# A Strassen unit in each branch projection, banded attention folded into one block, one-instruction gelu

## The chip, the cores and the metric

The program runs on one core of a Trainium2 chip. Its time is device microseconds of that core, from the runs shown beside the kernel; the profile is one further execution, recorded instruction by instruction. TensorE (PE) multiplies matrices into PSUM, VectorE (DVE) and ScalarE (ACT) do elementwise work, GpSimd (POOL) small work and some transfers, and SyncE (SP) issues most transfers from main memory.

## The reference

Two layers, 256 positions, width 2048, all in float32. Cut to what is computed:

```python
for l in range(DEPTH):                                  # 2
    h = rms_norm(x, mix_norm[l])                        # x: 256 x 2048
    q, k, v, uv, gate_logits = split(h @ w_in[l])       # 1024, 256, 256, 2048, 4096 columns
    q = apply_rope(rms_norm(q, q_norm[l])); k = apply_rope(rms_norm(k, k_norm[l]))
    # 16 query heads and 4 key heads of 64; a query sees the 128 positions up to itself
    a = sliding_window_attention(q, k, v, sinks[l]) @ w_attn_branch[l]      # 1024 x 2048
    u, v = split(gelu(uv))                              # gelu in its tanh form
    v = layer_norm of v in 8 groups of 128
    b = (u * (tril(w_spatial) @ v + bias)) @ w_sgu_branch[l]                # 1024 x 2048
    g = sigmoid(gate_logits)
    x = x + (g[:, :2048] * a + g[:, 2048:] * b) @ w_out[l]
    h2 = rms_norm(x, ffn_norm[l])
    x = x + (silu(h2 @ w_gate[l]) * (h2 @ w_up[l])) @ w_down[l]             # 5632 wide
```

In a block of 128 queries, query i sees the keys j > i of the block before and j <= i of its own: exactly one of the two for each j.

## The kernel before

The 256 positions are two tiles of 128. Every large product goes over *chunks* of 512 output columns, and within a chunk over *halves* of the weight, 256 rows by 512 columns (one 512 KB load). A number is carried as a sum of two fp32r parts: ACT makes `whi` from the loaded half (line 244), DVE makes `wlo` as the rest (line 245), and the left side has `uh` and `ul` in the same way. Each product of 128 rows takes three matmuls, `uh*whi`, `uh*wlo`, `ul*whi` (lines 340 and 341), so a half for both position tiles is 12 matmuls of 512 columns.

Most chunks run as pairs (`pair`). In the first 512 rows of a pair (unit `WINO`, in some pairs two units) the 2x2 blocks are multiplied by a Strassen scheme: seven products P1 to P7 of 6 matmuls in place of eight, at the price of three differences of weights (line 229), seven splits instead of four, sums of the left side (`sums`, split into `sh` and `sl` by the function `finished`, lines 501 to 505) and the copies and additions of lines 362 to 371. The head of a pair (its P products but P3) is interleaved with the last halves of the plan ahead of it. Before the change the in-projection, the output projection, and both parts of the feed-forward have such pairs; the two branch projections, 1024 rows to 2048 columns each, run as four single chunks each.

The list `entries` fixes the order of all halves and products. `Stream.next` runs ahead of it: loads up to seven entries ahead on SP's queue, differences six, splits four ahead into four `hi` and four `lo` buffers. PE's order is the order written; the other engines are ordered by a planner that has a timeline of its own. `tick()` passes once for each 12 matmuls (one *slot*); `after(n, fn)` has `fn` issued n slots later, behind the latest split on DVE. All smaller work is placed by such numbers: attention scores 17 slots after the first half of the queries is there, and so on.

Tiles of 4 KB a partition (left sides, gates, queries, sums, P5's `kept`) come from one pool, `big`, of 25; a tile is given back when its last reader is done. PSUM has four banks for products (`ps_acc`), two for transposes (`ps_tr`) and two for attention (`ps_at`).

A left side is made by `transposed`: DVE transposes 32x32 blocks into a `box` (line 410; one box, a pool of its own), 16 transfers gather it into `tt` (line 416, on POOL's or SP's queue), and ACT and DVE split it (lines 435 and 436, or the steps of `wino`, placed by tuples such as `WINO_HID`). Some go through PE instead (line 453).

Attention (class `Attention`): `scores` multiplies keys by queries (line 754; 128 key columns for the first tile of positions, 256 for the second), adds the mask (758), takes the maximum (762), and ACT takes the exponentials (771). Five slots later `weights` transposes them on PE (783) and ACT copies them out (785); three slots later `values` multiplies by V (793), with the weights as stationary side and 64 columns of V moving, and DVE divides by the sum (797). The result `att` is transposed by `transposed`. Gelu (`Spatial.gelu`, lines 816 to 822) is a square, two DVE instructions and a tanh, on half of the value.

Of the kernel before, what the change touches and what calls it, by code (L numbers as in the profile page):

```python
# [38 lines left out]
WINO_HID = 7, 8, 17, 18, 19, 20  # L39
# [5 lines left out]
TT = 1  # L45
K_TURN = 7
Q_TURN = 7
Q_FIRST = 17
Q_STEP = 5
# [4 lines left out]
GELU_A = 0.044715  # L54
GELU_C = 0.7978845608028654
# [3 lines left out]
def hybrid_trunk(ctx: ExitStack, tc: tile.TileContext, x, mix_norm, w_in, q_norm, k_norm, sinks,  # L59
# [6 lines left out]
    big = ctx.enter_context(tc.tile_pool(name="big", bufs=25))  # L66
# [3 lines left out]
    turned = ctx.enter_context(tc.tile_pool(name="turned", bufs=TT))  # L70
# [26 lines left out]
    class Plan:  # L97


        def __init__(self, key, head, body):  # L100
            self.key, self.head, self.body = key, head, body
            self.left = len(head) + len(body)
            self.paired = bool(head)
# [17 lines left out]
    def single(key, w):  # L121

        return Plan(key, [], [half(w, h, "X") for h in range(w.shape[0] // (2 * P))])

    def pair(key, wa, wb, by_unit=False, last_later=False, two=False):
# [25 lines left out]
        if last_later:  # L151
            body = g[:3] + p3 + g[3:4] + u[:2] + g[4:] + u[2:]
# [7 lines left out]
    plans = []  # L160
    for l in range(DEPTH):
# [21 lines left out]
    for p in plans:  # L183
        if p.head:
            h, n = p.head, min(6 if len(p.head) == 6 else 9, len(ahead.body))
# [5 lines left out]
            elif n == 6:  # L191
                order = [t[0], h[0], t[1], h[1], t[2], t[3], h[3], h[2], t[4], h[4], t[5], h[5]]
            else:
                order = [h[0], t[0], h[1], t[1], h[3], h[2], t[2], h[4], t[3], h[5]]
            if n != 9:
# [7 lines left out]
    class Stream:  # L203
# [7 lines left out]
        def load(self, upto):  # L211
            while self.asked < min(upto, len(entries)):
                for key, w, h, tag in entries[self.asked]["loads"]:
                    raw = (slot([P, 2, CW], name="raw") if tag == "slot" else
                           wraw.tile([P, 2, CW], F32, tag=tag, name=nm("raw"), bufs=None if tag == "raw" else 1))
                    src = w[2 * h * P:2 * (h + 1) * P, :].rearrange("(k p) n -> p k n", p=P)
                    if self.raws:
                        self.loaded = nc.sync.dma_start(raw, src)
                    else:
                        for i in range(2):  # L220
                            self.loaded = nc.sync.dma_start(raw[:, i:i + 1], src[:, i:i + 1])
# [101 lines left out]
    def banks(p, which):  # L323
        if which not in p.acc:
            other = p.paired and p.key[0] != "in" and which == "a"
# [77 lines left out]
    def turn(dst, src, queue):  # L403


        box = turned.tile([P, 4, 4, NT, B], F32, tag="box", name=nm("box"))
# [103 lines left out]

    class Norm:
# [42 lines left out]
    for c in range(NCH):  # L554
# [4 lines left out]
    mask = const.tile([P, S], F32, name="mask")  # L559
    nc.gpsimd.memset(mask, 0.0)  # L560
    nc.gpsimd.affine_select(mask[:, :P], mask[:, :P], pattern=[[1, P]], base=0, channel_multiplier=-1,
                            compare_op=ALU.is_gt, fill=-1e30)
    nc.gpsimd.affine_select(mask[:, P:], mask[:, P:], pattern=[[-1, P]], base=0, channel_multiplier=1,
                            compare_op=ALU.is_ge, fill=-1e30)
    cs = const.tile([P, NT, HD // 2], F32, name="cs")
# [97 lines left out]
    def fetch_large(pl):  # L663
        for n, i in ((13, 2), (17, 3), (21, 0), (25, 1)):
            after(n, lambda i=i: pl.fetch(i))
        after(40, pl.spatial)

    class Attention:


        def __init__(self, pl):
            self.pl = pl
            self.qT = [None] * 2
            self.att = [None] * 2
            self.attT = [None] * 2
            self.live = {}
# [38 lines left out]
        def keys(self, kv):  # L715
# [4 lines left out]
            after(K_TURN, lambda: turn(self.kT, kd.rearrange("p t n a d -> p t (n a d)"), nc.sync))  # L720

        def queries(self, c, q):
            self.rotate(q, NQ // 2, self.pl.rope[0], None)
            self.qT[c] = slot([P, 4, S], name="qT")
            self.att[c] = slot([P, NT, CW], name="att")
            after(Q_TURN, lambda: self.turn_queries(c, q))
            n = Q_FIRST + (4 * Q_STEP - 8) * c
            for t in range(NT):
                for g in (2 * c, 2 * c + 1):
                    after(n, lambda t=t, g=g: self.scores(t, g))  # L730
                    n += Q_STEP
            after(n + 6, lambda: transposed(self.attT, c, self.att[c], queue=nc.sync))
# [12 lines left out]
        def scores(self, t, g):  # L745
            nk = P * (t + 1)
            mk = mask[:, P:] if t == 0 else mask
# [295 lines left out]
```

## Time and profile before

| | us |
|---|---|
| median of 3 runs | 2461.22 (2460.16 to 2461.9) |
| the profiled execution | 2457.45 |
| its span, first to last instruction | 2455.7 |
| PE busy in the span | 2438.1 (99%) |
| DVE busy | 1999.5 (81%) |
| ACT busy | 1472.5 (60%) |

A group of instructions is given as line, engine, operation, output<-inputs, shape, count, then busy time, mean ns of one, and the idle time ahead of it with what ended it. Matmuls are pipelined: one lasts some 390 ns from start to end, but the next starts well before, so the pace is read from starts. DMA moved 506.74 MB, a mean of 206 GB/s.

### The profile page before, as it was taken

To read this page: it belongs to the slowest core of one execution; us is meant where nothing else is said; L and a number is where in the kernel's file an instruction comes from. 1 tells how busy PE (TensorE), PEld (TensorE's weight loads), DVE (VectorE), ACT (ScalarE), POOL (GpSimd) and SP (SyncE) were. 2 spreads that over 40 slices of the span, in tenths; PEclk is the share of its full clock that TensorE was granted. 3 is DMA by queue.
4 is the path that set the end of the run, shared out by engine and by line. 5 is a ranking of instruction groups with operands and counts; after the bars stand their busy time and mean duration, and the time that the engine had idled before them with its cause. 6 is when DMAs were issued, how large, how long until landed. Compare 5 with 4: busy or idle time off the path is not lost.

```text
span 2455.7 us, 31363 instructions
## 1 busy us (share of the span) xinstructions
PE 2438.1 (99%) x10968; PEld 2012.6 (82%) x10968; DVE 1999.5 (81%) x2320; ACT 1472.5 (60%) x1842; POOL 315.6 (13%) x592
## 2 busy tenths in 40 slices
PE   9999999999999999999999999999999999999999
PEld 7888888888888888887887888888888888888877
DVE  6798676797978997899877986768878789978996
ACT  5567544576655665566655665545666556655664
POOL 3100002132210111001101000021322101110110
PEclk9999999999999999999999999999999999999999
DMA  9555657576667657665747446675767675667654
GB/s 299 196 187 163 212 198 220 186 236 210 220 217 233 210 176 231 230 203 170 229 155 257 152 157 223 202 215 177 246 202 236 204 245 189 200 209 241 203 179 139
DMA packets 280782, 506.74 MB, mean 206 GB/s; under 512 B 28272, under 2 KB 40144, under 8 KB 280624
## 3 DMA queue, kind: packets, MB, share of 16 engines
q1 hardware_dynamic: 262544, 486.35, 61.0%
q0 software_dynamic: 17760, 18.12, 2.8%
q8 instruction: 86, 1.41, 0.2%
q14 instruction: 72, 0.59, 0.1%
q10 hardware_dynamic: 320, 0.27, 0.0%
HBM read 475.27 MB, written 2.10 MB: 194 GB/s over the span
## 4 chain that ended last, share of the span: by engine, by line
PE 90%; DVE 3%; DMA 3%; SPq 1%; issue 1%; ACT 1%; DVEq 0%; ACTq 0%
PE acc L340 59%; PE acc L341 29%; DMA raw<-in_w_in_dram 2%; DVE wlo L245 2%; SPq L416 1%; ACT whi L244 1%; PE po L793 1%; PE psc L754 0%; PE ppt L783 0%; DVE raw L229 0%; PE psg L871 0%; PE pt L453 0%; DMA raw<-in_w_up_dram 0%; DMA raw<-in_w_down_dram 0%; DVE box L410 0%
## 5 line engine op out<-in xcount | busy, mean ns | idle before, releaser
L244 ACT ACTIVATE whi<-raw 128x1024 fp32r<-128x1024 f32 (+1 forms) x1074 | 1132.0, 1059 | 883.0 <-PE acc L341 623.4
L245 DVE TENSOR_TENSOR wlo<-raw,whi 128x1024 fp32r<-128x1024 f32 (+1 forms) x1075 | 1301.3, 1219 | 399.0 <-ACT whi L244 386.7
L340 PE MATMUL acc<-whi,uh 128*128 128x512 f32 x2994 | 1170.3, 391 | 1.2 <-ACT uh L439 1.2
L340 PE MATMUL acc<-wlo,uh 128*128 128x512 f32 x2994 | 1167.1, 390 | 3.0 <-DVE wlo L245 2.9
L341 PE MATMUL acc<-whi,ul 128*128 128x512 f32 x2994 | 1166.4, 390 | 0.0
L340 PEld LDWEIGHTS acc<-wlo,uh 128*128 128x128 f32 x2994 | 562.6, 188 | 123.2 <-DVE wlo L245 6.0
L340 PEld LDWEIGHTS acc<-whi,uh 128*128 128x128 f32 x2994 | 562.6, 188 | 117.7 <-ACT uh L439 1.4
L341 PEld LDWEIGHTS acc<-whi,ul 128*128 128x128 f32 x2994 | 562.3, 188 | 117.8 <-DVE ul L444 0.5
L416 POOL DMA_DIRECT2D tt<-box x544 | 266.5, 497 | 1697.0 <-ACT whi L244 695.5
L229 DVE TENSOR_TENSOR raw<-raw,raw 128x1024 f32<-128x1024 f32 x236 | 287.8, 1219 | 1.6 <-DMA raw<-in_w_up_dram 0.8
L341 PE MATMUL acc<-whi,sl 128*128 128x512 f32 x472 | 184.0, 390 | 3.2 <-DVE sl L485 3.2
L340 PE MATMUL acc<-whi,sh 128*128 128x512 f32 x472 | 184.8, 392 | 1.7 <-ACT acc L364 1.7
L340 PE MATMUL acc<-wlo,sh 128*128 128x512 f32 x472 | 184.2, 390 | 0.0
L341 PEld LDWEIGHTS acc<-whi,sl 128*128 128x128 f32 x472 | 88.6, 188 | 22.5 <-DVE sl L485 4.0
L340 PEld LDWEIGHTS acc<-whi,sh 128*128 128x128 f32 x472 | 88.6, 188 | 20.9 <-ACT acc L364 2.1
L340 PEld LDWEIGHTS acc<-wlo,sh 128*128 128x128 f32 x472 | 88.7, 188 | 18.0
L366 DVE TENSOR_TENSOR kept<-acc,kept 128x512 f32<-128x512 f32 x94 | 64.3, 684 | 10.1 <-PE acc L341 10.1
L369 ACT ACTIVATE acc<-kept 128x512 f32<-128x512 f32 x94 | 54.9, 586 | 4.3 <-DVE kept L366 4.2
L888 DVE SCALAR_TENSOR_TENSOR xs<-acc,xs 128x512 f32<-128x512 f32 (+1 forms) x66 | 42.0, 668 | 8.4 <-PE acc L341 8.1
L436 DVE TENSOR_TENSOR ul<-tt,uh 128x512 fp32r<-128x512 f32 x52 | 34.0, 684 | 2.9 <-ACT uh L435 2.9
L435 ACT ACTIVATE uh<-tt 128x512 fp32r<-128x512 f32 x52 | 29.8, 618 | 9.4 <-DMA tt<-box 9.4
L312 POOL TENSOR_TENSOR rv<-ve,neg_half 128x4 f32<-128x4 f32 x8 | 11.9, 1486 | 172.9 <-DVE ve L839 159.5
(137 smaller groups left out, 874.8 us busy)
## 6 DMA issues: line engine op xcount, KB each, us to landing
raw<-in_w_in_dram SPq DMA_DIRECT2D x239, 512.0 KB, 4.7
raw<-in_w_gate_dram SPq DMA_DIRECT2D x176, 512.0 KB, 4.4
raw<-in_w_up_dram SPq DMA_DIRECT2D x176, 512.0 KB, 4.9
raw<-in_w_down_dram SPq DMA_DIRECT2D x176, 512.0 KB, 5.0
raw<-in_w_out_dram SPq DMA_DIRECT2D x64, 512.0 KB, 5.0
tt<-box POOLq DMA_DIRECT2D x544, 32.0 KB, 4.2
raw<-in_w_attn_branch_dram SPq DMA_DIRECT2D x32, 512.0 KB, 5.6
raw<-in_w_sgu_branch_dram SPq DMA_DIRECT2D x32, 512.0 KB, 4.4
```

The costliest lines, as they stand in the source:

```text
L229: self.last = nc.vector.tensor_tensor(out=self.raws[d], in0=self.raws[x], in1=self.raws[y], op=ALU.subtract)
L244: self.high = nc.scalar.activation(hi[:, i, :], raw[:, i, :], AF.Copy)
L245: self.last = nc.vector.tensor_tensor(out=lo[:, i, :], in0=raw[:, i, :], in1=hi[:, i, :].bitcast(F32), op=ALU.subtract)
L340: nc.tensor.matmul(ps, a, part[:, kk, :], start=first and kk + n == 0, stop=False, skip_group_check=True)
L341: nc.tensor.matmul(ps, b, hi[:, kk, :], start=False, stop=kk == 1, skip_group_check=True)
L366: nc.vector.tensor_tensor(out=p.kept[:, int(tag == "P7"), :], in0=a[1], in1=p.kept[:, 1, :], op=ALU.add)
L369: nc.scalar.activation(ps, p.kept[:, t, :], AF.Copy)
L416: q.dma_start(dst[j * B:(j + 1) * B, i], box[i * B:(i + 1) * B, j])
L435: nc.scalar.activation(h, s_, AF.Copy)
L436: nc.vector.tensor_tensor(out=l, in0=s_, in1=h.bitcast(F32), op=ALU.subtract)
L793: nc.tensor.matmul(po[:, h, :], pT[kb][:, h, :], self.kv[:, kb, KVW + g * HD:KVW + (g + 1) * HD], start=kb == 0, stop=kb == t)
L888: nc.vector.scalar_tensor_tensor(out=xs[:, t, sl], in0=sums[t][:, i * w:(i + 1) * w], scalar=scale, in1=xs[:, t, sl], op0=ALU.mult, op1=AL ...
```

## The change

- **Strassen in the branches.** The first two chunks of the attention branch become a pair, and so do those of the gating branch. The left side of the attention branch gets its Strassen sums in a new function `summed`, that of the gating branch through `transposed` with `WINO_FIRST`. Gate chunks 5 and 6 now run ahead of the gating branch's pair.
- **Attention.** For the second tile of positions the two key blocks are merged into one block of 128: ACT copies the own block's scores, DVE overwrites with the earlier block's where the mask says so. Maximum, exponentials and transposes work on 128 columns for either tile. The weights are divided by their sum while untransposed. `values` takes 64 columns of V as the stationary side and moves 512 columns (4 heads) of transposed weights; two key heads write the lower and the upper 64 rows of one PSUM bank. V of the second block is replaced by its difference to the first, and the weights are multiplied by a 0/1 mask for that product. The result is already transposed, so `transposed` falls away; the rows of `w_attn_branch` are loaded in the order of heads that this gives, in two transfers for a half (`rows_of`).
- **Gelu** is one ACT instruction a tile (`Gelu_apprx_tanh`), four in a row for v and four for u, chained behind the exponentials on ACT.
- **Boxes** come from `big`, which has 26 tiles, and the pool `turned` is gone.
- **Placement.** New slots for scores, values, gelu, the mixing with `w_spatial` and its transposes (now 34 slots into a layer, 40 before); queues and delays of some `transposed` calls; Strassen sums of the last feed-forward round end 15 slots after the turn (`WINO_END`) and not 20.

```diff
-WINO_HID = 7, 8, 17, 18, 19, 20
+WINO_HID = 11, 12, 17, 18, 19, 20
+WINO_END = 9, 10, 12, 13, 14, 15
...
-Q_FIRST = 17
-Q_STEP = 5
+W_TURN = 9
+SCORES = (17, 22, 27, 32), (37, 42, 47, 52)
+V_GELU, V_STEP = 4, 6
+U_GELU, U_MIX, U_TURN = 2, (3, 9), (32, 39)
+VALUES = (34, 44), (54, 64)
...
-    big = ctx.enter_context(tc.tile_pool(name="big", bufs=25))
+    big = ctx.enter_context(tc.tile_pool(name="big", bufs=26))
...
+    def rows_of(raw, w, h):
+        if w.shape[0] != QW or not any(w is a for a in by_heads):
+            return [(raw, w[2 * h * P:2 * (h + 1) * P, :].rearrange("(k p) n -> p k n", p=P))]
+        rows = w.rearrange("(c a k d) n -> c a d k n", c=2, a=2, d=HD)
+        k = 2 * (h % 2)
+        return [(raw[a * HD:(a + 1) * HD], rows[h // 2, a, :, k:k + 2]) for a in range(2)]
...
         if last_later:
-            body = g[:3] + p3 + g[3:4] + u[:2] + g[4:] + u[2:]
+            body = g[:2] + p3 + u[:2] + g[2:] + u[2:]
...
-        plans += [single(("att", l), w) for w in cols_of(w_attn_branch[l], NCH)]
-        sgu = [single(("sgu", l), w_sgu_branch[l, :, j * CW:(j + 1) * CW]) for j in range(NCH)]
-        plans += [sgu[0], pair(("in", l), of_in("gate", 5), of_in("gate", 6)), sgu[1], sgu[2],
-                  single(("in", l), of_in("gate", 7)), sgu[3]]
+        plans += [pair(("att", l), c_[0], c_[1])] + [single(("att", l), w) for w in c_[2:]]
+        plans[-3].first = True
+        c_ = cols_of(w_sgu_branch[l], NCH)
+        plans += [pair(("in", l), of_in("gate", 5), of_in("gate", 6)), pair(("sgu", l), c_[0], c_[1]),
+                  single(("in", l), of_in("gate", 7)), single(("sgu", l), c_[2]), single(("sgu", l), c_[3])]
...
-        box = turned.tile([P, 4, 4, NT, B], F32, tag="box", name=nm("box"))
+        box = slot([P, 4, 4, NT, B], name="box")
...
+    def summed(units, c, at):
+        uh, ul = units[c]
+        flat = slot([P, 4, S], name="flat")
+        nc.vector.tensor_tensor(out=flat, in0=uh.bitcast(F32), in1=ul.bitcast(F32), op=ALU.add)
+        ss = slot([P, 4, 2, P], name="sums")
...
-        after(40, pl.spatial)
+        after(34, pl.spatial)
...
-                nc.vector.tensor_tensor(out=pr[:, :, j, :nk], in0=pscore[:, :, :nk],
-                                        in1=mk.unsqueeze(1).to_broadcast([P, 2, nk]), op=ALU.add)
+                mk = mask.unsqueeze(1).to_broadcast([P, 2, P])
+                if t == 0:
+                    nc.vector.tensor_tensor(out=pr[:, :, j, :], in0=pscore[:, :, :P], in1=mk, op=ALU.add)
+                else:
+                    nc.scalar.activation(pr[:, :, j, :], pscore[:, :, P:], AF.Copy)
+                    nc.vector.copy_predicated(pr[:, :, j, :], mk.bitcast(mybir.dt.uint32), pscore[:, :, :P])
...
-            after(5, lambda: self.weights(t, g, pr4, rd))
+            after(4, lambda: nc.vector.tensor_tensor(out=pr4, in0=pr4, in1=rd.unsqueeze(2).to_broadcast([P, 4, P]),
+                                                     op=ALU.mult))
+            after(W_TURN, lambda: self.weights(t, g, pr4))
...
+            nc.scalar.activation(pT[0][:, g % 2], pt, AF.Copy)
+            if t == 1:
+                nc.vector.tensor_tensor(out=pT[1][:, g % 2], in0=pt, in1=causal.unsqueeze(1).to_broadcast([P, 4, P]),
+                                        op=ALU.mult)
...
+            po = ps_at.tile([P, 4, P], F32, tag="at", name=nm("po"))
+            pT = self.pT[t, c]
+            for k in range(t + 1):
+                for a in range(2):
+                    v = (1 - k) * KVW + (2 * c + a) * HD
+                    nc.tensor.matmul(po[a * HD:(a + 1) * HD], self.kv[:, 0, v:v + HD], pT[k][:, a],
+                                     start=k == 0, stop=k == t)
+            uh, ul = (x[:, :, t * P:(t + 1) * P] for x in units)
+            nc.scalar.activation(uh, po, AF.Copy)
+            nc.vector.tensor_tensor(out=ul, in0=po, in1=uh.bitcast(F32), op=ALU.subtract)
...
+            last = self.att.exps
+            for dst in both:
+                for t in range(NT):
+                    with tc.issue_after(last.ins):
+                        last = nc.scalar.activation(dst[:, t, :], dst[:, t, :], AF.Gelu_apprx_tanh)
...
-                pe, soon = c == len(hT) - 1 == 2, c == 3
+                pe, soon = c == len(hT) - 1 == 2, c == 3 or c == 1 and len(hT) == 3
```

More of the change, by code (lines that the diff above doesn't have):

```diff
@@ L324, in banks @@
         if which not in p.acc:
-            other = p.paired and p.key[0] != "in" and which == "a"
+            other = p.paired and p.key[0] != "in" and which == "a" and not p.first
             if other or p.key[0] == "in":
@@ L940, in hybrid_trunk, with gated @@
         for chunks in FIRST_PART[l]:
+            if chunks == FIRST_PART[l][-1]:
+                after(1, lambda: summed(att.attT, WINO, (1, 2, 4)))
             projected(*chunks)
-        for j in range(NCH):
-            ps = product(("att", l))
+        def gated(j, ps):
             ga = gates[j]
@@ L949, in hybrid_trunk @@
                                                op0=ALU.add, op1=ALU.mult)
+        product_pair(("att", l), lambda ps: gated(0, ps), lambda ps: gated(1, ps))
+        for j in range(2, NCH):
+            gated(j, product(("att", l)))
             tick()
```

173 lines of the change are left out of this document (93 added, 80 removed).

## The prediction

> **What bounds the kernel now.** I read the page first, its busy times and the chain that ended last, then the groups by form, then TensorE's waits, and last single stretches of the timeline. The page's first lines and its chain:
>
> ```profile
> span 2455.7 us, 31363 instructions
> PE 2438.1 (99%) x10968; PEld 2012.6 (82%) x10968; DVE 1999.5 (81%) x2320; ACT 1472.5 (60%) x1842; POOL 315.6 (13%) x592
> PE 90%; DVE 3%; DMA 3%; SPq 1%; issue 1%; ACT 1%; DVEq 0%; ACTq 0%
> ```
>
> TensorE is busy for 99% of the span and carries 90% of the chain, so time changes by what its queue loses or gains, and by its waits. A matmul lasts 390 ns but overlaps the next one, so I take the pace from starts, in a quiet stretch of the timeline of TensorE:
>
> ```profile
> 599.78 0.39 PE L341 MATMUL acc<-whi,ul 128*128 128x512 f32 x1
> ...
> 611.80 0.39 PE L340 MATMUL acc<-wlo,uh 128*128 128x512 f32 x1
> ```
>
> From the first to the last of these are 53 steps in 12.02 us: 0.2268 us for a matmul of the large products. Counting the lists of the code gives 10398 of these, 2358 us of the span. The other 98 us are attention, transposes, the start and waits. TensorE's longest waits in total (us, times, longest):
>
> ```profile
> PE acc L341 <- DVE sl L485: 3.2, 2, 1.6
> PE acc L340 <- DVE wlo L245: 2.9, 5, 0.8
> PE ppt L783 <- DVE wsT L654: 2.4, 1, 2.4
> PE acc L340 <- ACT acc L364: 1.7, 1, 1.7
> PE acc L340 <- ACT uh L439: 1.2, 1, 1.2
> ```
>
> They are short: no engine but TensorE bounds a stage for long. The nearest to it is DVE in the attention stretch, as the table by windows shows (columns: PE, PEld, DVE, ACT, POOL busy, granted clock, DMA share, GB/s):
>
> ```profile
> 140.00:160.00 20.00, 20.00 (x100) 16.40 (x99) 19.97 (x39) 12.77 (x22) 4.09 (x2) 1.00 0.47 145
> 280.00:300.00 20.00, 20.00 (x90) 16.39 (x89) 10.18 (x11) 8.83 (x11) 0.00 (x0) 1.00 0.65 221
> 340.00:360.00 20.00, 20.00 (x90) 16.53 (x90) 16.45 (x17) 11.16 (x12) 0.00 (x0) 1.00 0.39 120
> 1340.00:1360.00 20.00, 17.57 (x86) 14.41 (x85) 16.80 (x32) 12.76 (x23) 0.51 (x1) 0.91 0.55 192
> ```
>
> **The change part by part**, on TensorE first. All sums are made against the profiled execution, 2457.45 us (span 2455.7); the median of the runs, 2461.2, lies 3.8 above it, which I add at the end.
>
> *Strassen.* A pair replaces eight products of 6 matmuls by seven. Two more pairs in each of two layers: 4 x 6 = 24 matmuls fewer, 24 x 0.2268 = **-5.4**.
>
> *Transposes of the weights.* For the second tile of positions each group of 8 becomes one of 4. The group of lines of `values`, and the timeline of TensorE:
>
> ```profile
> L793 PE MATMUL po<-kv,pT 128*128 128x64 f32 x192 | 23.1, 270 | 0.0
> ```
>
> ```profile
> 134.00 0.66 PE L783 MATMUL ppt<-ident,pr 128*128 128x128 f32 x4
> ...
> 149.16 1.14 PE L754 MATMUL psc<-kT,qT 64*128 64x256 f32 x8
> 150.24 1.09 PE L783 MATMUL ppt<-ident,pr 128*128 128x128 f32 x8
> ...
> 249.93 1.02 PE L871 MATMUL psg<-v,wsT 128*128 128x256 f32 x4
> ```
>
> A group of 8 takes 1.09, of 4 0.66; there are 8 such groups: 8 x 0.43 = **-3.5**. The scores keep their matmuls.
>
> *Weights times V.* Now 23.1 us busy in 16 groups. After it there are 12 matmuls of 512 moving columns in each layer (4 for the first tile, 8 for the second, over the two query chunks), each recorded as two passes, as every float32 product here. Four passes of 256 columns took 1.02 us at line 871, of which 0.16 is the tail that the next product overlaps (as in the first rows, 0.39 long and 0.23 apart): 0.215 a pass, so 0.43 for 512 columns. 48 passes are 20.6 us one after another, about 21.8 with the tails of 8 groups: -1.3. But each matmul uses half of the array's columns, and the two key heads use different halves. No row shows column halves. The nearest row is the scores, line 754, on half of the rows: eight passes of 256 columns in 1.14 us, where four passes on the whole array took 1.02. So two halves ran side by side. By that the 48 passes take 10.3, with tails 11.5: **-11.6**. I take this end, because the scores are the only half-array products in the trace, and keep -1.3 for the range.
>
> The Trainium skill, "TensorEngine Tiling (Array Packing)", sections Tiling Modes and Performance Considerations, says that tiles of the array work independently and gives column tiling of 64 up to twofold speed, and that a change of tiling mode drains the engine. The scores' rows agree on row halves (1.14 beside 1.02); no run here shows column halves. By the page the term would be -11.6, by strict order -1.3.
>
> *Waits that go.* The wait for `wsT` lies at the start of layer 2: the transposes of `w_spatial` take both banks that the weights' transposes need. Slot 34 in place of 40 puts them 8 slots ahead of the first weights (scores at 33, plus 9). What the wait costs beside itself is in the timeline:
>
> ```profile
> 1345.03 0.66 PE L783 MATMUL ppt<-ident,pr 128*128 128x128 f32 x4 [2.43 <-DVE wsT L654]
> 1345.44 0.48 PE L340 MATMUL acc<-whi,uh 128*128 128x512 f32 x1
> ...
> 1349.40 0.40 PE L340 MATMUL acc<-wlo,uh 128*128 128x512 f32 x1
> ```
>
> Ten matmuls then take 3.96 us, not 2.27, and the granted clock of that window is 0.91: 2.43 + 1.69 = 4.1. The Trainium skill, "TensorE: Matmul & The Clock Gate", section Part 1, puts such a fall at idle windows of some 3.4 us. Here 2.43 us with short transposes around it was enough, so I charge any new wait of that size with 1.7 more.
>
> The two waits for `sl` (3.2) come from Strassen sums of the last feed-forward round that end in the very slot before P5 needs them; at 15 in place of 20 they end five slots, 13 us, earlier. The wait for `acc` (1.7) stands behind them: ACT held P5's copies behind a split that waited for the second hidden chunk's gather; that gather now starts a slot earlier and on two queues. Together **-9.0**. The waits for `wlo` (late loads) and at the start stay.
>
> *What is added off TensorE.* DVE, from these rows:
>
> ```profile
> L758 DVE TENSOR_TENSOR pr<-psc,mask 128x512 f32<-128x512 f32 x16 | 10.8, 682 | 2.1 <-PE psc L754 2.1
> L762 DVE TENSOR_REDUCE mx<-pr 128x4 f32<-128x1024 f32 x8 | 9.7, 1207 | 0.0
> L797 DVE TENSOR_TENSOR att<-po,rd 128x256 f32<-128x256 f32 x16 | 6.7, 416 | 0.8 <-PE po L793 0.8
> L410 DVE STREAM_TRANSPOSE box<-att 128x512 f32<-128x512 f32 x8 | 5.6, 704 | 0.0
> L819 DVE SCALAR_TENSOR_TENSOR sq<-sq,u 128x512 f32<-128x512 f32 x8 | 5.5, 686 | 2.6 <-ACT sq L818 2.6
> L762 DVE TENSOR_REDUCE mx<-pr 128x4 f32<-128x512 f32 x8 | 5.4, 675 | 0.0
> L229 DVE TENSOR_TENSOR raw<-raw,raw 128x1024 f32<-128x1024 f32 x236 | 287.8, 1219 | 1.6 <-DMA raw<-in_w_up_dram 0.8
> ```
>
> Per layer, gone: gelu 16 x 0.69 = 11.0; the turn of `att` 4 x 0.70, and 4 splits of its kind at 0.69, 5.6; line 797, 8 x 0.42 = 3.3; the shorter maximum 4 x 0.53 = 2.1. New: dividing 8 x 0.69 = 5.5, the masked copy 4 x 0.69, splitting the result 4 x 0.69, the difference of V 0.4, `summed` 2 x 1.22 + 4 x 0.42 = 4.1. The overwriting copy replaces the masked add of 682 ns; I bound it by 416 and 682, the same form at half and at full width. So attention and gelu free 6 to 9 us of DVE in a layer, just where it is full (19.97 of 20). Each pair adds 3 differences, 3 splits and 2 additions, 3 x 1.22 + 3 x 1.22 + 2 x 0.68 = 8.7, but later, where the same table has DVE at 10 and 16 of 20 (280 and 340 us); the in-projection's pairs bear as much. I cost both at nothing: covered by four splits of lead.
>
> ACT loses 8 instructions of gelu in a layer, and gains 3 splits and 4 copies a pair and table loads:
>
> ```profile
> L771 ACT ACT_TABLE_LOAD x1 | 1.3, 1283 | 0.0
> ```
>
> If gelu needs another table than exp and tanh, four gelus (0.69 each, as line 819 on DVE) are a block of 2 x 1.28 + 4 x 0.69 = 5.3 us, twice a layer, against a lead of three to four entries (4 to 10 us): nothing, or about 1 us each. Transfers: the branch weights come in 64 transfers in place of 32 (by the code); 64 gathers of `att` leave SP's queue and 48 for other turns come to it from POOL's. SP issues loads seven entries ahead, so 16 more in the whole span are nothing.
>
> *New waits.* `values` follows the scores by two slots (three before) and needs one of the two banks that the scores fill. In the timeline, scores and the masked adds that free the bank:
>
> ```profile
> 132.93 1.14 PE L754 MATMUL psc<-kT,qT 64*128 64x256 f32 x8
> ...
> 135.00 0.68 DVE L758 TENSOR_TENSOR pr<-psc,mask 128x512 f32<-128x512 f32 x1
> ```
>
> ```profile
> 115.37 0.72 PE L754 MATMUL psc<-kT,qT 64*128 64x128 f32 x8
> ...
> 122.81 0.75 DVE L758 TENSOR_TENSOR pr<-psc,mask 128x256 f32<-128x256 f32 x2
> ```
>
> The bank came free 2.8 us after the scores began in the one case and 8.2 in the other (behind a late load). `values` comes 1.1 + 2 x 2.72 = 6.5 us behind, six times in all: from 0 up to 1.7 each, with the clock's 1.7 in the worst. Bounds 0 and 20; I take 3 for these and the gelu blocks, near the first row.
>
> Sum: -5.4 - 3.5 - 11.6 - 9.0 + 3 = -26.5, so 2431 for a profiled execution and **2435** as a median.
>
> **The rivals.** *A: the column halves do not pair.* Then 10.3 less is gained: 2445. For it: no row shows them, and each half needs all 128 rows of its own moving side. Against: line 754.
>
> *B: the old waits are only exchanged.* If `sl`, `acc` and `wsT` come back elsewhere, or every `values` waits at its bank, 9 to 15 us are given back: about 2447. For it: two slots instead of three. Against: DVE gets lighter there.
>
> *C: slower, because the pool of large tiles runs out.* I count what is live in slot 73, when the second half of u is written: left sides 10, gates 2, kv 1, v and u 4, layer norm rows 2, `w_spatial` 1, weights 2, results of attention 4: all 26. One more, and ACT's copy of u out of PSUM waits until the last `values` (slot 81) gives tiles back. ACT then makes no splits, and TensorE stops when its lead of 4 to 8 us is used up: 8 slots x 2.72 - 6 = 16 us in each layer, plus the clock: 2435 + 2 x (16 + 1.7) = 2470. It decides from a wait of seven to eight slots on; below, the gain outweighs it. Against it: my count ends at 26, not 27, and the layer norm rows come free one slot later.
>
> **How the numbers follow.** 0.2%, 4.9 us, is about what a measurement of this kernel can tell from no change. Forecast 0.45 (its own range 2428 to 2441), A 0.27, B 0.15, C 0.09, and 0.04 for a mixture of A and B that ends within 0.2%. Faster: 0.45 + 0.27 + 0.14 = 0.86; slower, C: 0.09; within: 0.05. The range reaches from the forecast without new waits and with a few old ones gone as well, 2428, over A and B to 2458.
>
> **What would show it.** Main matmuls at lines of `add_product` 10374; 64 transposes of weights; `values` with 48 passes, about 0.21 us apart if they pair and 0.43 if not; no wait for `wsT`, `sl` or `acc`; DVE below 19 of 20 us in 140 to 160; granted clock 1.00 from 1340 to 1360. The prediction is wrong if TensorE's waits grow beyond 15 us, above all ACT waiting for tiles near 190 and 1400 us, or if DVE's overwriting copy is much dearer than 0.7 us.

## The result, and the profile after

| | before | after |
|---|---|---|
| median of the runs shown together, us | 2460.99 (2460.16 to 2461.9) | 2427.85 (2427.18 to 2428.32) |
| ratio to before, 95% interval | | 0.9865 [0.985, 0.9881] |
| profiled execution, us | 2457.45 | 2427.18 |
| its span, us | 2455.7 | 2425.5 |

The change makes the kernel 33 us faster (29 to 37 by the interval); between the two profiled executions the difference is 30.3. The page of the changed kernel, its span, busy times and the chain that ended last:

```profile
span 2425.5 us, 31042 instructions
PE 2417.2 (100%) x10768; PEld 1984.1 (82%) x10768; DVE 2025.9 (84%) x2346; ACT 1492.1 (62%) x1878; POOL 290.7 (12%) x545
PE 96%; DMA 2%; DVE 1%; issue 0%; ACT 0%; POOL 0%; SPq 0%; DVEq 0%; ACTq 0%
```

TensorE carries 96% of the chain in place of 90%: what is left is nearly all its own queue. DVE has 26 us more to do than before (the prediction's rows for attention, gelu and pairs add up to 17 to 23), and that costs nothing visible. TensorE's waits, all that the view lists (us in total, times, longest):

```profile
PE acc L353 <- DVE wlo L258: 2.0, 4, 0.8
PE pwarm L304 <- DVE warm L299: 1.1, 1, 1.1
PE acc L353 <- ACT uh L452: 0.9, 1, 0.9
PE pt L466 <- DVE xs L950: 0.3, 1, 0.3
```

They come to 4.3 us; the list of before came to 13.5. The waits for `sl`, `acc` and `wsT` are gone, and no new one stands in the list. The groups of the attention's transposes (835), products with V (850) and of the overwriting copy (807):

```profile
L850 PE MATMUL po<-pT,kv 128*64 128x512 f32 x48 | 12.1, 609 | 0.0
L835 PE MATMUL ppt<-ident,pr 128*128 128x128 f32 x64 | 9.6, 272 | 0.0
L807 DVE COPY_PREDICATED pr<-mask,psc 128x256 f32<-128x256 uint32 x16 | 6.4, 443 | 0.0
```

The 48 passes are busy 12.1 us, where the products with V were busy 23.1; the 64 transposes 9.6. One group of `values` in the timeline of TensorE:

```profile
184.20 1.94 PE L850 MATMUL po<-pT,kv 128*64 128x512 f32 x8
```

Eight passes in 1.94 us. One after another, at 0.43 each, they would take 3.4; two side by side take four times 0.43, and 0.2 for the tail. So the two column halves work at the same time. Busy time by windows (length of the window, then PE, PEld, DVE, ACT, POOL, granted clock, DMA share, GB/s):

```profile
140.00:160.00 20.00, 20.00 (x96) 15.21 (x94) 17.40 (x23) 15.06 (x28) 0.00 (x0) 1.00 0.71 213
180.00:200.00 20.00, 20.00 (x91) 14.74 (x92) 19.87 (x38) 13.86 (x25) 1.01 (x1) 1.00 0.35 98
1340.00:1360.00 20.00, 20.00 (x95) 16.02 (x95) 17.99 (x26) 13.53 (x25) 0.00 (x0) 1.00 0.52 153
```

DVE has slack at 140 to 160 us (17.40, before 19.97), but is as full as ever 40 us later (19.87, before 19.63), and TensorE waits in neither window. At 1340 the clock stays at 1.00.

Put side by side, the two profiles give: 24 matmuls fewer, 5.4; transposes 13.8 to 9.6 us busy, 4.2; products with V 23.1 to 12.1, 11.0; waits 13.5 to 4.3, 9.2; and the slowed clock behind the `wsT` wait, 1.7. That is 31.5 of a span shorter by 30.2; 1.3 go the other way and are not placed.

### The profile page after: what moved, and what is told of

Its sections match the earlier page's. It is cut to its first block, busy times and chain, and to the rows that moved or that the text cites. A ratio compares the mean times of both kernels' runs of the same rounds, so it can differ in the third digit from the quotient of the medians.

```text
span 2425.5 us, 31042 instructions
## 1 busy us (share of the span) xinstructions
PE 2417.2 (100%) x10768; PEld 1984.1 (82%) x10768; DVE 2025.9 (84%) x2346; ACT 1492.1 (62%) x1878; POOL 290.7 (12%) x545
## 4 chain that ended last, share of the span: by engine, by line
PE 96%; DMA 2%; DVE 1%; issue 0%; ACT 0%; POOL 0%; SPq 0%; DVEq 0%; ACTq 0%
PE acc L353 63%; PE acc L354 31%; DMA raw<-in_w_in_dram 2%; PE psc L798 1%; PE po L850 0%; DVE wlo L258 0%; PE psg L933 0%; PE ppt L835 0%; ACT whi L257 0%; PE pt L466 0%; POOL rq L325 0%; DVE ul L457 0%; SPq L290 0%; DVE xs L950 0%; DVE box L423 0%
## 5 line engine op out<-in xcount | busy, mean ns | idle before, releaser
L258 DVE TENSOR_TENSOR wlo<-raw,whi 128x1024 fp32r<-128x1024 f32 (+1 forms) x1087 | 1314.9, 1219 | 344.5 <-ACT whi L257 329.1
L353 PE MATMUL acc<-whi,uh 128*128 128x512 f32 x2954 | 1154.5, 391 | 0.9 <-ACT uh L452 0.9
L353 PE MATMUL acc<-wlo,uh 128*128 128x512 f32 x2954 | 1150.7, 390 | 2.0 <-DVE wlo L258 2.0
L354 PE MATMUL acc<-whi,ul 128*128 128x512 f32 x2954 | 1150.0, 389 | 0.0
L429 POOL DMA_DIRECT2D tt<-box x496 | 243.0, 497 | 1632.2 <-DVE box L423 747.5
L242 DVE TENSOR_TENSOR raw<-raw,raw 128x1024 f32<-128x1024 f32 x252 | 307.4, 1220 | 1.7 <-DMA raw<-in_w_up_dram 0.8
L353 PE MATMUL acc<-whi,sh 128*128 128x512 f32 x504 | 197.9, 393 | 0.0
L353 PE MATMUL acc<-wlo,sh 128*128 128x512 f32 x504 | 196.5, 390 | 0.0
L379 DVE TENSOR_TENSOR kept<-acc,kept 128x512 f32<-128x512 f32 x102 | 69.8, 684 | 10.3 <-PE acc L354 10.3
L376 ACT ACTIVATE kept<-acc 128x512 f32<-128x512 f32 x51 | 30.3, 594 | 8.4 <-PE acc L354 7.9
L820 ACT ACTIVATE pr<-pr,negm 128x128 f32<-128x128 f32 x64 | 24.9, 389 | 14.1 <-DVE negm L811 14.1
```

The lines of the kernel that those rows point to most:

```text
L242: self.last = nc.vector.tensor_tensor(out=self.raws[d], in0=self.raws[x], in1=self.raws[y], op=ALU.subtract)
L258: self.last = nc.vector.tensor_tensor(out=lo[:, i, :], in0=raw[:, i, :], in1=hi[:, i, :].bitcast(F32), op=ALU.subtract)
L353: nc.tensor.matmul(ps, a, part[:, kk, :], start=first and kk + n == 0, stop=False, skip_group_check=True)
L354: nc.tensor.matmul(ps, b, hi[:, kk, :], start=False, stop=kk == 1, skip_group_check=True)
L376: nc.scalar.activation(p.kept[:, 1, :], a[0], AF.Copy)
L379: nc.vector.tensor_tensor(out=p.kept[:, int(tag == "P7"), :], in0=a[1], in1=p.kept[:, 1, :], op=ALU.add)
```

## Experiments

Each edit is against the changed kernel, but for one that starts from the kernel before. Ratios are to the kernel before on the same chip.

**The Strassen pairs undone.** All chunks of both branches are single again; attention, gelu and placement stay.

```diff
-        plans += [pair(("att", l), c_[0], c_[1])] + [single(("att", l), w) for w in c_[2:]]
-        plans[-3].first = True
+        plans += [single(("att", l), w) for w in c_]
...
-        plans += [pair(("in", l), of_in("gate", 5), of_in("gate", 6)), pair(("sgu", l), c_[0], c_[1]),
+        plans += [pair(("in", l), of_in("gate", 5), of_in("gate", 6)), single(("sgu", l), c_[0]), single(("sgu", l), c_[1]),
...
```

> The changed kernel with the two branches as single chunks again, so 24 matmuls of the large products more. Theory (TensorE bounds, the pairs' extra work on DVE and ACT is covered): 24 x 0.2268 = 5.4 us slower than the changed kernel, about 2433, the added busy time of DVE gone and TensorE's waits unchanged. Rival (the pairs' splits and sums cost TensorE waits): less than 3 us slower, or faster, and fewer waits of TensorE.

Measured: 2435.51 us (2434.93 to 2436.21), ratio 0.99 [0.9887, 0.9914]; 7.7 above the changed kernel. The 24 matmuls are 5.4 of it, and a wait accounts for the rest: TensorE's longest in this run, and what DVE did just ahead of it, in the timeline:

```profile
PE acc L352 <- DVE kept L378: 2.0, 2, 1.0
```

```profile
344.32 0.70 DVE L422 STREAM_TRANSPOSE box<-u 128x512 f32<-128x512 f32 x1
344.95 0.65 DVE L378 TENSOR_TENSOR kept<-acc,kept 128x512 f32<-128x512 f32 x1
```

The addition that the pair of gate chunks 5 and 6 waits for stands behind a turn of u. So the pairs give their 5.4; taking them out also makes that wait of 1 us in each layer, which the changed kernel does not have. The theory holds for the 5.4; that TensorE's waits stay as they are, which it also said, does not.

**The kernel before, with only the waits taken away.** To the kernel before, three placements: `w_spatial` at slot 34, the last round's sums at 15, its second hidden chunk gathered earlier on two queues.

```diff
+WINO_END = 9, 10, 12, 13, 14, 15
-        after(40, pl.spatial)
+        after(34, pl.spatial)
-                pe, soon = c == len(hT) - 1 == 2, c == 3
+                pe, soon = c == len(hT) - 1 == 2, c == 3 or c == 1 and len(hT) == 3
...
-                      lambda: transposed(hT, c, hid, on_pe=pe, wino=WINO_HID if c == WINO else None,
-                                         queue=None if soon else nc.gpsimd, late=-2 if soon else 0))
+                      lambda: transposed(hT, c, hid, on_pe=pe, wino=None if c != WINO else WINO_HID if len(hT) == 4 else WINO_END,
+                                         queue=None if soon else nc.gpsimd, late=-2 if c == 3 else 0))
```

> The kernel before with only two placements of the change: w_spatial's transposes at slot 34, and the last round's Strassen sums at 15 slots with the second hidden chunk turned a slot earlier on two queues. Theory: the waits for wsT, sl and acc go, with the slowed clock behind the first, 9.0 us faster than before, about 2452; no wait above 1 us in TensorE's list but those for late loads and the start. Rival B of the prediction (waits are only exchanged): less than 4 us faster, with new names in that list.

Measured: 2449.85 us (2448.56 to 2452.48), ratio 0.996 [0.9947, 0.9972], 10.1 below the kernel before in the same runs (2459.95). Its three longest waits:

```profile
PE acc L341 <- DVE wlo L246: 2.3, 4, 0.8
PE acc L341 <- ACT uh L440: 1.4, 1, 1.4
PE acc L341 <- DVE kept L367: 1.3, 2, 0.9
```

`sl`, `acc` and `wsT` are gone from the old kernel too, at the price of 1.3 for `kept`. On the kernel before, these three placements together are worth 10 us by the medians and 7.6 between the profiled executions (span 2448.1 against 2455.7).

**The last sums put back.** Strassen sums of the last feed-forward round 20 slots after the turn, its second hidden chunk on POOL's queue.

```diff
-WINO_END = 9, 10, 12, 13, 14, 15
+WINO_END = 7, 8, 17, 18, 19, 20
-                pe, soon = c == len(hT) - 1 == 2, c == 3 or c == 1 and len(hT) == 3
+                pe, soon = c == len(hT) - 1 == 2, c == 3
```

> The changed kernel with the last round's Strassen sums at 20 slots again and the second hidden chunk turned as before. Theory: the two waits for sl come back, 3.2 us, and the one for acc, 1.7: 3 to 5 us slower than the changed kernel, 2431 to 2433. Rival (with lighter DVE they would have gone anyway): within 1 us of it.

Measured: 2436.09 us (2434.76 to 2438.13), ratio 0.9903 [0.989, 0.9917]; 8.2 above the changed kernel, where 3 to 5 were expected. The two waits, and the two windows in which they lie:

```profile
PE acc L353 <- ACT acc L377: 3.4, 2, 1.7
PE acc L354 <- DVE sl L498: 3.2, 2, 1.6
```

```profile
1140.00:1160.00 20.00, 16.74 (x72) 12.91 (x71) 17.68 (x20) 13.45 (x16) 3.91 (x8) 1.00 0.52 149
...
2350.00:2370.00 20.00, 16.74 (x64) 12.76 (x63) 16.21 (x17) 12.35 (x15) 2.27 (x5) 0.91 0.48 145
```

Both waits now come in both layers (before, `acc` came only in the second): 6.6 us. In both windows TensorE idles 3.26 us, but only in the second is the clock down, and TensorE begins 64 matmuls in place of 72, 1.8 us of work at 0.2268 each. The kernel before has the same idle 3.26 us at 2370 to 2390 with the clock at 1.00 and 71 matmuls. The Trainium skill, "TensorE: Matmul & The Clock Gate", section Part 1, has the activity window run freely, not started by the kernel; equal gaps with unequal clocks fit that, but no run here shows where the window lay. Its idle window of some 3.4 us is longer than any single gap here (1.7), and yet the clock fell.

**`w_spatial` at its old slot.**

```diff
-        after(34, pl.spatial)
+        after(40, pl.spatial)
```

> The changed kernel with w_spatial's transposes at slot 40 again. Theory (the wait hung on two sets of transposes sharing two banks): the weights now come at slot 42, two slots behind, so DVE has some 5 us for the copies; a wait of 0 to 2.5 us comes back in one layer or both, with the clock's 1.7 if it is long: 0 to 5 us slower. Rival (the wait was ACT's and DVE's delay by a late gather, whatever the slot): no wait at the weights' transposes, time within 1 us.

Measured: 2427.89 us (2427.38 to 2429.64), ratio 0.9868 [0.9853, 0.9883]: no difference to the changed kernel. All that TensorE waits for `wsT`:

```profile
PE ppt L835 <- DVE wsT L695: 0.2, 1, 0.2
```

So slot 34 is not what removes the wait in the changed kernel. The rival of the expectation, that the wait was only DVE's delay by a late gather, is answered by the timeline of DVE at the start of layer 2, before the change and in this run:

```profile
1341.80 2.57 DVE L245 TENSOR_TENSOR wlo<-raw,whi 128x1024 fp32r<-128x1024 f32 x2 [5.75 <-ACT whi L244]
1344.29 1.28 DVE L654 COPY wsT<-pw 128x512 f32<-128x512 f32 x2
```

```profile
1332.54 1.23 DVE L258 TENSOR_TENSOR wlo<-raw,whi 128x1024 fp32r<-128x1024 f32 x1 [6.19 <-ACT whi L257]
1335.42 1.28 DVE L695 COPY wsT<-pw 128x512 f32<-128x512 f32 x2
```

DVE's delay is there in both, 5.75 and 6.19 us, behind ACT, which had waited for a gather. What differs is when TensorE wants the banks back: in the kernel before, the weights' transposes stand right behind those of `w_spatial` and one group of scores (their wait ends at 1345.03, in the middle of the copies); they come only at 1345.21 in this run, 8.5 us after the copies. So a late gather alone does not make the wait. In the changed kernel the weights follow the scores by nine slots instead of five. In the kernel before the wait is gone with slot 34 too (the run above, though that run has the other placements as well).

**The products with V done twice.** The whole list of passes is repeated. The sum is started anew at each k = 0 (`start=k == 0`), so the second round replaces the first, and the attention's result is not doubled, though the expectation says so. The passes added are those that it counts.

```diff
-            for k in range(t + 1):
+            for k in [k for _ in range(2) for k in range(t + 1)]:
```

> The changed kernel with every product of weights and V done a second time and added to the first, so that the attention result is doubled; the time alone is of interest. Theory (column halves run side by side, and no matmul of 512 columns in float32 costs more than its share): 24 more pairs of passes at 0.43, 10.3 us slower than the changed kernel, about 2438. Rival A (each pass by itself): 20.6 us slower, about 2448.

Measured: 2439.09 us (2438.37 to 2440.64), ratio 0.9919 [0.9905, 0.9933]; 11.2 above. The group:

```profile
L850 PE MATMUL po<-pT,kv 128*64 128x512 f32 x96 | 22.4, 601 | 0.0
```

48 passes more add 10.3 us busy. Column halves pair, and rival A falls.

**`values` one slot after the scores.** The bank that it needs then has 2.7 us less to come free.

```diff
-VALUES = (34, 44), (54, 64)
+VALUES = (33, 43), (53, 63)
```

> The changed kernel with values one slot behind the scores in place of two (33, 43, 53, 63). The bank that it needs came free 3.8 to 5.4 us after the scores began; at one slot TensorE reaches values 3.5 to 3.8 us after them. Theory (two slots are just enough, which is why no wait came): waits at po of 0.1 to 1.9 us in six places, 2 to 8 us slower in all, 2430 to 2436. Rival (the bank is no constraint, the planner hurries the copies): no wait, within 1 us.

Measured: 2428.6 us (2427.87 to 2429.13), ratio 0.9875 [0.9862, 0.9889]; 0.75 above, with ratio intervals that overlap the changed kernel's, and less than the 2 to 8 us of the theory. One wait at the bank:

```profile
PE po L850 <- DVE pr L807: 0.7, 1, 0.7
```

Even a slot earlier, one group in eight waits, for 0.7 us. The bank is not what limits `values`.

**One large tile less.**

```diff
-    big = ctx.enter_context(tc.tile_pool(name="big", bufs=26))
+    big = ctx.enter_context(tc.tile_pool(name="big", bufs=25))
```

> The changed kernel with 25 tiles in the large pool in place of 26. Theory (rival C of the prediction, one tile too few near slot 73): ACT or DVE waits for a tile, TensorE stands still in each layer, 10 us or more slower than the changed kernel. Rival (tiles come free a little earlier than counted): within 2 us of it.

Measured: 2435.41 us (2434.55 to 2437.62), ratio 0.9896 [0.988, 0.9913]; 7.6 above. TensorE's wait, ACT in the timeline, and TensorE behind the wait:

```profile
PE acc L353 <- ACT u L869: 6.1, 1, 6.1
```

```profile
240.38 1.26 ACT L869 ACTIVATE u<-acc,rstd 128x512 f32<-128x512 f32 x2 [4.18 <-DVE v L914]
```

```profile
241.71 0.63 PE L353 MATMUL acc<-wlo,uh 128*128 128x512 f32 x1
242.13 0.63 PE L354 MATMUL acc<-whi,ul 128*128 128x512 f32 x1
242.56 0.63 PE L353 MATMUL acc<-whi,uh 128*128 128x512 f32 x1
```

ACT stands at the copy of u's second half until DVE's multiplication of v by the layer norm's row (914) lets that row's tile go, and TensorE follows. So rival C's mechanism stands one tile away from the kernel as it is, at the instruction that it named. But the tile comes from the layer norm's rows, which C had as its counterargument, and not from the last `values`: the wait lasts 6 us, not 16, and comes in one layer of two. Behind it nine matmuls take 3.87 us and not 2.04, starting some 0.43 us apart: 1.8 us more, about what the prediction charged for the clock.

**The old gelu in the new places.** The square, two DVE instructions and tanh again, in place of one ACT instruction.

```diff
-                        last = nc.scalar.activation(dst[:, t, :], dst[:, t, :], AF.Gelu_apprx_tanh)
...
+                    nc.scalar.activation(sq, xh, AF.Square, scale=2.0)
+                    nc.vector.scalar_tensor_tensor(out=sq, in0=sq, scalar=1.0 / 0.044715, in1=xh,
+                                                   op0=ALU.add, op1=ALU.mult)
+                    nc.scalar.activation(sq, sq, AF.Tanh, scale=2.0 * 0.7978845608028654 * 0.044715)
+                    nc.vector.scalar_tensor_tensor(out=xh, in0=sq, scalar=1.0, in1=xh, op0=ALU.add, op1=ALU.mult)
```

> The changed kernel with the old gelu (a square, a tanh and two DVE instructions for each tile) at the new places: 11 us of DVE more in a layer, no change of ACT's tables. Theory (DVE's work in the attention stretch is covered by the splits' lead): within 2 us of the changed kernel. Rival (the freed DVE time is why no new wait came): 3 to 10 us slower, with waits for wlo or at the banks between 150 and 240 us.

Measured: 2429.89 us (2429.06 to 2430.05), ratio 0.9874 [0.986, 0.9889]; 2.0 above, with ratio intervals that overlap the changed kernel's. DVE is busy 2041.9 us there and 2025.9 in the changed kernel: 16 us of its work in the attention stretch are worth about 2, if anything: it is not clear of the noise.

**More pairs.** First, both pairs of chunks in both branches:

```diff
-        plans += [pair(("att", l), c_[0], c_[1])] + [single(("att", l), w) for w in c_[2:]]
-        plans[-3].first = True
+        plans += [pair(("att", l), c_[0], c_[1]), pair(("att", l), c_[2], c_[3])]
+        plans[-2].first = plans[-1].first = True
...
-                  single(("in", l), of_in("gate", 7)), single(("sgu", l), c_[2]), single(("sgu", l), c_[3])]
+                  single(("in", l), of_in("gate", 7)), pair(("sgu", l), c_[2], c_[3])]
```

> The changed kernel with the last two chunks of either branch as a pair as well: 24 matmuls fewer. Theory: 5.4 us faster than the changed kernel, about 2422.5, if the third and fourth chunk of the gating branch, whose results now come later and together, still reach the output projection in time. Rival (they come late): TensorE waits for uh of a merged chunk at the start of the output projection, 2 to 8 us in each layer, so equal or slower.

Measured: 2458.57 us (2457.36 to 2460.3), ratio 0.9999 [0.999, 1.0008]: 31 us lost, with 24 matmuls fewer, where 5.4 gained were expected. Second, only the attention branch (the lines above the dots):

> The same for the attention branch alone: 12 matmuls fewer, nothing moved after it. Theory: 2.7 us faster than the changed kernel, about 2425, with no new wait. Rival (pairs crowd DVE, which bears two of them behind each other here): less than 1 us faster, with waits for wlo.

Measured: 2459.91 us (2458.27 to 2462.93), ratio 1.0006 [0.9997, 1.0015]. Here 2.7 gained were expected, and 32 us are lost: the attention branch's second pair is enough for all of the loss. TensorE's two longest waits, and the instruction on DVE at the first long stall:

```profile
PE acc L353 <- ACT acc L377: 14.8, 4, 4.3
PE acc L353 <- ACT whi L257: 5.5, 2, 5.0
```

```profile
315.14 1.22 DVE L242 TENSOR_TENSOR raw<-raw,raw 128x1024 f32<-128x1024 f32 x1 [4.16 <-DMA raw<-in_w_attn_branch_dram]
```

DVE stood 4.16 us for weights of the attention branch, and ACT and TensorE behind it; the same comes in layer 2 (4.25 us of DVE at 1536). All waits of TensorE in this run come to 27.2 us, 22.9 more than in the changed kernel. The clock adds to them: the mean granted clock of the profiled execution is 0.995 (1.000 in the changed kernel), and 0.83 in the windows of 20 us from 440 and from 1560. These weights come in two transfers of 64 partitions each. The next two kernels load them whole.

**Whole loads.** Heads of equal parity go to the same column half, so that the rows of `w_attn_branch` keep their order; the products with V become twice as many of 256 columns, with the same work.

```diff
-            for k in range(t + 1):
-                for a in range(2):
+            for a in range(2):
+                for k in range(t + 1):
+                    for i in range(2):
...
-        if w.shape[0] != QW or not any(w is a for a in by_heads):
+        if True:
```

> The changed kernel with heads of equal parity in one column half, so that the rows of the attention weights lie in their given order and each tile loads in one transfer of 512 KB instead of two of 256 KB on 64 partitions each: 32 transfers instead of 64 for them. Theory (the split transfers cost time only where loads are late, and no load is late in the changed kernel): within 2 us of the changed kernel, 2427 to 2430. Rival (the halved transfers already cost the attention stage some us that don't show as waits): 3 us or more faster.

Measured: 2428.02 us (2426.98 to 2428.57), ratio 0.9873 [0.9858, 0.9888]: no difference. In the windows one sees what differs all the same, with the split loads (the changed kernel) and with the whole ones:

```profile
300.00:320.00 20.00, 20.00 (x90) 16.58 (x89) 13.54 (x15) 10.68 (x12) 0.00 (x0) 1.00 1.03 244
```

```profile
300.00:320.00 20.00, 20.00 (x90) 16.53 (x89) 13.57 (x15) 11.22 (x13) 0.00 (x0) 1.00 0.78 261
```

The same stretch moves 244 GB/s with the DMA engines fully busy (share 1.03), or 261 with 0.78 of them. In this window 14 of the 16 loads issued with the split are halves for the attention branch. The Trainium skill, "DMA: Bandwidth & Descriptors", section Rules for kernel authors, advises against two transfers to disjoint halves of the partitions, as both use the same DMA engines, and gives no price; here it is 335 GB/s per full share whole and 237 split. In this kernel it costs no time, as nothing waits.

The same with the attention branch's second pair:

> The kernel with both pairs of the attention branch as Strassen units (2459.91 us), with the same whole 512 KB loads of the attention weights. Theory (part of its loss is late loads: SyncE spent 27.75 us issuing 21 of the split ones from 284.5 us on, and TensorE stood 4.4 us at 315): the waits at about 315 and 1540 us go, and the time falls by 10 us or more, to below 2450. Rival (the loss is that VectorE and ScalarE can't make two units' operands in this place, whatever the loads do): the waits of some 4 to 5 us at about 449, 541 and 1568 stay, those at 315 and 1540 too, and the time stays within 5 us of 2460.

Measured: 2451.11 us (2449.55 to 2452.89), ratio 0.9968 [0.9956, 0.9981], 8.8 below the same pairs with split loads (9 by the ratios): a little less than the ten and the 2450 that the theory asked for. The stall at 315 is gone, as is that in layer 2; a wait of 1.4 us for `kept` stands near either place instead. TensorE's three longest waits, and ACT and DVE ahead of the stall of 4.0 us that stays at 443:

```profile
PE acc L353 <- ACT acc L377: 6.3, 2, 4.0
PE acc L353 <- ACT whi L257: 4.7, 2, 4.3
PE acc L353 <- DVE kept L379: 4.6, 5, 1.4
```

```profile
445.61 1.06 ACT L257 ACTIVATE whi<-raw 128x1024 fp32r<-128x1024 f32 x1 [3.84 <-DVE raw L242]
```

```profile
439.68 1.22 DVE L258 TENSOR_TENSOR wlo<-raw,whi 128x1024 fp32r<-128x1024 f32 x1
440.82 0.70 DVE L423 STREAM_TRANSPOSE box<-gate 128x512 f32<-128x512 f32 x1
441.44 0.65 DVE L1026 TENSOR_TENSOR gate<-gate,gate 128x512 f32<-128x512 f32 x1
442.02 2.34 DVE L258 TENSOR_TENSOR wlo<-raw,whi 128x1024 fp32r<-128x1024 f32 x2
444.28 1.21 DVE L242 TENSOR_TENSOR raw<-raw,raw 128x1024 f32<-128x1024 f32 x1
```

Without a gap DVE makes splits and turns of the gates, reaches the difference of weights (242) at 444.28, and ACT idles 3.84 us for it: at 443 the theory on DVE is shown. The other two long stalls have other causes. ACT ahead of the one of 2.3 us at 535, then DVE and SP's queue ahead of the one of 4.3 us at 1555:

```profile
534.91 1.06 ACT L257 ACTIVATE whi<-raw 128x1024 fp32r<-128x1024 f32 x1 [1.66 <-PE acc L354]
535.87 0.58 ACT L376 ACTIVATE kept<-acc 128x512 f32<-128x512 f32 x1
536.48 0.58 ACT L377 ACTIVATE acc<-acc 128x512 f32<-128x512 f32 x1
```

```profile
1557.37 1.23 DVE L242 TENSOR_TENSOR raw<-raw,raw 128x1024 f32<-128x1024 f32 x1 [5.88 <-DMA raw<-in_w_in_dram]
```

```profile
1543.24 10.01 SPq L429 DMA_DIRECT2D tt<-box  x16
1553.35 1.03 SPq L231 DMA_DIRECT2D raw<-in_w_in_dram  x2
```

At 535 ACT's copies of P5 stand behind a split that had itself waited for TensorE, and TensorE waits for the copies. At 1555 DVE idles 5.88 us for weights of the in-projection, which always come whole: the last loads of them ahead of that were issued behind 16 gathers that held SP's queue for 10 us. That these gathers made the load late is read from the order and was not tested. So both theories hold a part: late split loads cost 8.8 us, and of what is left one stall is DVE's work, one ACT's order and one a late load of another kind. How much of the 32 us each is worth beyond its wait, with the clock, was not separated. No kernel of this study is faster than the changed one.

## Why the prediction was right or wrong

The direction and the mechanism were right; 2435 was 7.15 us too high, and 2427.85 lies 0.15 outside the lower end of 2428. Point by point:

- **Strassen, -5.4: right.** 10374 large matmuls are in the trace, as forecast. Undoing it cost 7.7, of which 2.0 was a wait that the undoing made. That the extra differences and splits are covered holds for these pairs and not in general: a second pair in the attention branch lost 32 us.
- **Transposes of the weights, -3.5: right,** 4.2 by busy time; no run tested it by itself.
- **Weights times V, -11.6 with column halves side by side: right.** 11.0 by busy time; doubling the passes cost 11.2, where rival A needed 20.6. The reading from the scores' row halves carried over. The Trainium skill, "TensorEngine Tiling (Array Packing)", section Key Properties, has tiles working independently, and the trace now agrees for column halves.
- **Waits that go, -9.0: right in size.** The same steps on the kernel before gave 10.1 by the medians and 7.6 between profiled executions, which is what the sum was made of. One of the reasons was wrong: in the changed kernel the `wsT` wait goes without slot 34, since the weights now come nine slots behind the scores. And the last sums were worth more than the 4.9 of their waits: putting them back cost 8.2.
- **DVE and ACT at nothing: right for time.** DVE is at 17.40 of 20 at 140 to 160, below 19 as forecast, but at 19.87 at 180 to 200, so the attention stretch is not freed as a whole. The overwriting copy takes 443 ns, near the lower bound of 416. The gelu of one instruction is worth about 2 us, not clear of the noise.
- **New waits, +3: the step that failed in the sum.** None came. I had taken the wait for the PSUM bank from the spread of 2.8 to 8.2 us before; `values` placed a slot earlier still waits only once, 0.7 us. And 1.9 us of old waits went that I had left standing: `psc` behind `att` (0.7, the instruction is gone), and parts of those for `wlo` and `uh`, about which nothing was tested. The terms above differ by 0.1 together, so by terms that is 5.0 us below the forecast; the 1.3 that aren't placed go against it, and the sum was 3.8 too high, profile to profile (-30.3 against -26.5).
- **From the profile to the median, +3.8: the other step that failed.** I carried the distance of one profiled execution from its median over as if it belonged to the kernel. The changed kernel's profiled execution lies 0.7 below its median; this is 3.1 of the 7.15. Part of the 3.8 was chance: the 46 executions of the kernel before beside the experiments have a median of 2459.0 (2457.1 to 2463.3), 2.2 below the median of three that I started from. The executions with a lower clock are the longer ones: the seven of the 46 with a mean granted clock of 0.996 or 0.997 took 2461.2 to 2463.3, those with 0.999 or 1.000 have a median of 2458.8. The four of the changed kernel, whose waits are shorter, have 0.999 or 1.000 and lie within 1.1 us of each other. That shorter waits also take slowed clock away from the median fits these numbers; no run separates it.
- **Rivals.** A is excluded by the doubled passes. B, old waits only exchanged, did not happen. C did not happen, but is one tile away: with 25 tiles its wait appears at the copy that the count of live tiles had named, at 235 us and not near 190, and 6 us long where 16 were counted.

The range failed by its low end: it allowed no new waits and "a few old ones gone as well", but still on top of the 3.8.

## What to carry to other kernels

Where one engine is busy for 99% of the span, what a change takes out of its queue can be summed from starts in a quiet stretch, and short waits are worth listing and removing one by one: three placements gave the kernel before 10 us. Adding the same good unit again is not free: the second pair in the attention branch, with 12 matmuls fewer, lost 32 us, 8.8 of it to late split loads and the rest to stalls with at least three causes and to the clock behind them. Stalls that look alike need to be followed one by one. A median should be forecast from the median of many runs, and not from one profiled execution plus its own distance.

## What the runs showed of the hardware

- Two matmul passes with 64 stationary columns each, on different halves of the array, run at the same time in float32: eight passes of 512 columns in 1.94 us.
- A wait of TensorE of 1.6 us and one of 1.7 within 20 us left the granted clock at 1.00 in one place and took it to 0.91 in another of the same execution.
- After a wait of 6.06 us, nine matmuls took 3.87 us in place of 2.04, starting some 0.43 us apart: 1.8 us lost beside the wait.
- A stretch made mostly of loads onto half of the partitions took about 1.4 times the DMA engines' time per byte (237 GB/s per full share, whole loads 335); the kernel's time was the same as long as no load was late.
